# Loading and storing token tiles: one transfer over 128 partitions in place of four over 32

## The chip, the cores and the metric

The kernel runs on one core of a Trainium2 chip. The metric is the time of one execution on the device, in microseconds. The engines are named as in the profile: PE is TensorE (matmul), PEld its weight loads, DVE VectorE, ACT ScalarE, POOL GpSimd, SP the sync engine. In this kernel every transfer is issued by SP, and SP's own sequencer stands in the profile as SPq.

## What is computed

Two layers of a backbone over 1024 latent tokens and 256 context tokens of width 1024, in float32. Layer 0 is differential attention with rotary positions, layer 1 a bidirectional S5 state-space mixer with a GLU; each is followed by a squared-ReLU MLP of width 4096. Sublayers are wrapped in RMS norms and in shift, scale and gate from adaLN. Context reads only context; latent tokens read both. Cut to what matters here:

```python
for i in range(2):
    sh1, s1, g1, sh2, s2, g2 = split(silu(c) @ ada_w[i] + ada_b[i], 6)      # and the same from c_ctx for the context
    h = rmsnorm(x, norm_g[i, 0]) * (1 + s1) + sh1
    y = diff_attention(h, ...) if i == 0 else s5_mixer(h, ...)
    x = x + g1 * rmsnorm(y, norm_g[i, 1])
    h = rmsnorm(x, norm_g[i, 2]) * (1 + s2) + sh2
    x = x + g2 * rmsnorm(square(relu(h @ w1[i])) @ w2[i], norm_g[i, 3])
return x                                                                    # (1, 1024, 1024)
```

## The kernel before

The 1280 tokens stand in ten tiles of 128: tiles 0 to 7 are latent tokens, 8 and 9 context. A tile does not hold 128 neighbouring tokens. A token's number is written as c, sh (0 to 3) and sl (0 or 1), with token = 8 c + 2 sh + sl. Tiles 2p and 2p + 1 are a pair; the pair takes 32 values of c, and tile i takes sl = i mod 2. Partition 32 sh + j of a tile holds the j-th c of its pair with that sh. So the 32 rows for one sh are 8 tokens apart in DRAM, and the four blocks of 32 partitions start 2 tokens apart. A row of one token is 4 KB; in a pair both sl stand next to each other, so its rows are 8 KB.

Two helpers move such rows. `pair_dma` loads a pair, for `v_norm` at the start of the kernel. `tile_dma` loads or stores one tile of 128 rows. Each issues four transfers, one for each sh, of 32 partitions. All transfers of the kernel go through `self.dma` (L80), which issues them from SP in one queue.

The callers, in order of time:

- `v_norm` (called from `phase_v`): pairs 0 and 1 are loaded first, then 2 and 3, then the context pair 4. The rows are normalised (ACT L149, POOL L336), transposed on PE (`to_feature`, L314), scaled and shifted by the adaLN columns and split in a high and a low part; `mm3` (L132 to L134) multiplies them as three matmuls. The adaLN products (L249, L204) and the projection of V run at the same time.
- `phase_c`, after attention: the output projection. For each tile (in the order 8, 9, 0 to 7) `finish` loads the residual rows of x, adds them to the normalised projection (L1273), stores the sum to DRAM as `xa`, and normalises it once more for the MLP (L149, L1280). Three buffers `xs` hold the rows, in turn, so the load for a tile waits until the tile three places earlier is stored and read. Feature transposes of a group need all four of its tiles.
- `m0_tile`, at the end of the first MLP: `first` loads the rows of `xa`, `residual` (L1644) adds them and, for the latent tiles, stores the sum to `xb`; `second`, `root` and `modulate` (L1652) norm it for the next layer and write over the stored rows in place. Then `transposed` (L1619) lays the rows out for the S5 mixer, whose first product is at L1727; S5 also reads tables (`ptd`, `recd`) through the same queue. `glu_done` later loads `xb` by a transfer of its own, which the change does not touch.

A planner orders each engine's instructions ahead of time (`schedule_with_timeline_sim`), and an engine works them off in that order. Eight semaphores are used in turn for the transfers, so a transfer is issued only when the one eight places earlier has landed.

Of the kernel before, what the change touches and what calls it, by code (L numbers as in the profile page):

```python
# [70 lines left out]
class Prog:  # L71
# [206 lines left out]
    def tile_dma(self, dram, i, slot, store=False):  # L278

        d = dram[1] if i >= 8 else dram[0]  # L280
        src = d.rearrange("(c sh sl) d -> sl sh c d", sh=4, sl=2)[i % 2]
        if i < 8:
            src = src[:, 32 * (i // 2) : 32 * (i // 2) + 32]
        for sh in range(4):
            s = slot[32 * sh : 32 * sh + 32]
            if store:
                self.dma(src[sh], s)
            else:
                self.dma(s, src[sh])

    def pair_dma(self, dram, pair, slot):

        src = (dram[1] if pair == 4 else dram[0]).rearrange("(c sh sl) d -> sh c (sl d)", sh=4, sl=2)
        if pair < 4:
            src = src[:, 32 * pair : 32 * pair + 32]
        for sh in range(4):
            self.dma(slot[32 * sh : 32 * sh + 32].rearrange("p a b -> p (a b)"), src[sh])

    G_TOK = (512, 512, 256)
    G_TILES = ((0, 1, 2, 3), (4, 5, 6, 7), (8, 9))  # L300
# [1964 lines left out]
```

## Time and profile before

| | |
|---|---|
| median of 3 runs | 2943.51 us (2942.1 to 2946.0) |
| the profiled execution | 2951.44 us, span 2949.7 us |
| mean granted TensorE clock | 0.981 |
| PE, PEld, DVE, ACT, POOL busy | 95%, 78%, 64%, 44%, 34% of the span |
| transfers of SP's queue | 510.11 MB, 55.7% of 16 DMA engines' span |
| mean rate of all transfers | 174 GB/s |

How to read the lines that follow. A row of the stretches ("4.00:12.50 ...") gives the stretch in us from the span's start, its length, then busy us and (in brackets) instructions of PE, PEld, DVE, ACT and POOL, then the granted PE clock, the mean busy share of the 16 DMA engines and GB/s. A row of the timeline gives start, duration in us, engine, line, operation, out<-in, and in square brackets how long the engine had been idle and what released it. A row of one line's instructions gives count, then min/median/max in ns and the first and last start in us. A row of the waits gives who waited for whom, us in total, times and the longest. A row of the chain gives start, us, and the work that held the end.

### The profile page before, as it was taken

What the parts mean: (1) busy time and instruction counts of PE and PEld (TensorE: products, weight loads), DVE (VectorE), ACT (ScalarE), POOL (GpSimd) and SP (SyncE); (2) the same over time, 40 slices, a digit from 0 to 9 for tenths busy, and PEclk for the clock granted to TensorE, in tenths of its full rate; (3) what the DMA queues carried; (4) which work ended last, traced back from release to release, by engine and by line L of the source; (5) the groups of instructions that cost most, each with busy time, mean ns of one, the idle gap of its engine ahead of it and who ended that gap; (6) DMA issues with size and microseconds to landing.
All of it is one profiled execution on the core that took longest, in us unless ns stands there. A gap on an engine that the chain in (4) does not pass through costs nothing.

```text
span 2949.7 us, 44385 instructions
## 1 busy us (share of the span) xinstructions
PE 2795.1 (95%) x16040; PEld 2315.4 (78%) x16040; DVE 1877.9 (64%) x2777; ACT 1309.8 (44%) x2412; POOL 1016.2 (34%) x911
## 2 busy tenths in 40 slices
PE   6998999999899999999999999779899999999999
PEld 4687888888777887888777778678788778888887
DVE  5356788878763654444578764888633676658466
ACT  3424556555553743233422231357434655345443
POOL 2214676666653600000100001677301334326324
PEclk9999999999899999999999999989999999999999
DMA  9954455454625445322566674569934475467544
GB/s 269 300 193 141 129 156 154 153 156 146 217 86 177 138 152 185 125 97 86 194 173 186 183 238 119 150 184 278 287 121 154 151 234 189 151 205 263 161 137 140
DMA packets 422920, 512.95 MB, mean 174 GB/s; under 512 B 57142, under 2 KB 295980, under 8 KB 421548
## 3 DMA queue, kind: packets, MB, share of 16 engines
q1 hardware_dynamic: 422700, 510.11, 55.7%
q8 instruction: 126, 2.06, 0.3%
q14 instruction: 94, 0.77, 0.1%
HBM read 351.29 MB, written 154.50 MB: 171 GB/s over the span
## 4 chain that ended last, share of the span: by engine, by line
PE 55%; DVE 6%; DMA 5%; ACT 3%; issue 2%; SPq 2%; POOL 1%; DVEq 0%; POOLq 0%; ACTq 0%
PE PS L132 17%; PE PS L134 17%; PE PS L133 17%; SPq L80 2%; PE PS L1727 1%; DVE FD L1747 1%; DMA U<-in_ada_w 1%; DVE H L138 1%; DMA W<-in_mlp_w 1%; DMA H<-xb 1%; PE PS L204 1%; PE PS L1768 0%; ACT F L552 0%; DMA W<-recd 0%; DVE F L542 0%
## 5 line engine op out<-in xcount | busy, mean ns | idle before, releaser
L132 PE MATMUL PS<-H,R 128*128 128x512 f32 (+1 forms) x816 | 302.9, 374 | 8.3 <-DVE FC L468 5.8
L132 PE MATMUL PS<-H 128*128 128x512 f32 x768 | 300.3, 392 | 3.9 <-ACT H L137 3.9
L134 PE MATMUL PS<-H 128*128 128x512 f32 x768 | 299.4, 391 | 1.6 <-DVE H L138 1.6
L133 PE MATMUL PS<-H 128*128 128x512 f32 x768 | 300.8, 392 | 0.0
L133 PE MATMUL PS<-H,R 128*128 128x512 f32 (+1 forms) x816 | 293.9, 360 | 1.4 <-POOL H L138 1.4
L134 PE MATMUL PS<-H,R 128*128 128x512 f32 (+1 forms) x816 | 293.8, 361 | 0.0
L132 PE MATMUL PS<-R,H 128*128 128x512 f32 x540 | 217.5, 406 | 2.0 <-ACT R L137 1.4
L552 ACT ACTIVATE F<-F,stat 128x1280 f32<-128x1280 f32 x128 | 174.3, 1362 | 100.8 <-DVE F L542 100.6
L137 ACT ACTIVATE R<-W 128x512 fp32r<-128x512 f32 (+1 forms) x186 | 133.1, 721 | 193.2 <-PE PS L133 149.4
L134 PE MATMUL PS<-R,H 128*128 128x512 f32 x540 | 211.7, 396 | 1.8 <-DVE H L138 1.8
L133 PE MATMUL PS<-R,H 128*128 128x512 f32 x540 | 213.3, 396 | 0.0
L138 DVE TENSOR_TENSOR H<-W,H 128x512 fp32r<-128x512 f32 (+1 forms) x145 | 136.7, 951 | 109.6 <-ACT H L137 102.5
L542 DVE TENSOR_SCALAR_CACHE_REDUCE F<-PS 128x1280 f32<-128x1280 f32 x128 | 185.1, 1482 | 18.5 <-PE PS L517 18.5
L589 POOL TENSOR_SCALAR R<-F 128x256 fp32r<-128x256 f32 (+1 forms) x128 | 135.8, 1061 | 162.2 <-ACT F L588 144.6
L138 DVE TENSOR_TENSOR R<-W,R 128x512 fp32r<-128x512 f32 (+1 forms) x149 | 126.0, 851 | 102.9 <-ACT R L137 81.7
L137 ACT ACTIVATE H<-W 128x512 fp32r<-128x512 f32 (+2 forms) x166 | 107.1, 653 | 178.8 <-PE PS L133 117.9
L132 PEld LDWEIGHTS PS<-H,R 128*128 128x128 f32 x816 | 154.9, 190 | 37.2 <-DVE FC L468 7.4
L517 PE MATMUL PS<-R,R 64*128 64x256 f32 (+1 forms) x1380 | 160.4, 351 | 21.8 <-DVE F L542 7.5
L134 PEld LDWEIGHTS PS<-H,R 128*128 128x128 f32 x816 | 154.7, 190 | 26.4 <-POOL R L138 1.4
L133 PEld LDWEIGHTS PS<-H,R 128*128 128x128 f32 x816 | 155.5, 191 | 22.7 <-POOL H L138 1.7
L132 PEld LDWEIGHTS PS<-H 128*128 128x128 f32 x768 | 144.4, 188 | 36.5 <-ACT H L137 4.7
L134 PEld LDWEIGHTS PS<-H 128*128 128x128 f32 x768 | 144.5, 188 | 32.4 <-DVE H L138 2.1
(450 smaller groups left out, 7230.0 us busy)
## 6 DMA issues: line engine op xcount, KB each, us to landing
W<-in_mlp_w SPq DMA_DIRECT2D x192, 256.0 KB
Ad<-F SPq DMA_DIRECT2D x112, 256.0 KB
W<-Ad SPq DMA_DIRECT2D x112, 256.0 KB
W<-in_ada_w SPq DMA_DIRECT2D x32, 512.0 KB
W<-in_mlp_w SPq DMA_DIRECT2D x32, 512.0 KB
H<-hidd SPq DMA_DIRECT2D x64, 256.0 KB
U<-in_ada_w SPq DMA_DIRECT2D x32, 512.0 KB
W<-in_s_w_glu SPq DMA_DIRECT2D x64, 256.0 KB
```

Source lines behind the costliest of these rows:

```text
L80: return self.nc.sync.dma_start(out=out, in_=in_)
L132: mm(out, ah, bh, start=first, stop=False, **kw)
L133: mm(out, ah, bl, start=False, stop=False, **kw)
L134: mm(out, al, bh, start=False, stop=last, **kw)
L137: self.nc.scalar.activation(hi, src, AF.Copy)
L138: (lo_eng or self.nc.vector).tensor_tensor(lo, src, hi.bitcast(F32), ALU.subtract)
L204: self.nc.tensor.matmul(acc[32 * j : 32 * j + 32, 0:256], self.scT[:, 2 * k : 2 * k + 32], w[:, 256 * j : 256 * j + 256], start=k == 0, st ...
L517: mm(self.PS[:, o : o + k1 - k0], Q[rows, i, qs], K[j][rows, k0:k1], start=n == 0, stop=n == 2)
L542: ts(p[c], self.PS[:, 1280 * c : 1280 * c + 1280], 1.0, None, ALU.mult, ALU.min, accum_out=sm[:, c : c + 1])
L552: nc.scalar.activation(p[c], p[c], AF.Exp, bias=sm[:, c : c + 1], scale=-1.0, accum_out=sn[:, 0:1] if c else s0[:, u + 1 : u + 2])
L589: nc.gpsimd.tensor_scalar(hi, t, 1.0, 0.0, ALU.mult, ALU.add)
L1727: mm(b[:, o : o + 160], X[:, d, i, 64 * j : 64 * j + 128], U[:, 4 * n + i, cols], start=True, stop=True)
```

## The change

`tile_dma` and `pair_dma` issue one transfer for all 128 partitions. The DRAM side is a pattern of [4 values of sh][32 values of c][row], the SBUF side the whole buffer of 128 partitions. Buffers, callers and everything else stay as they are.

```diff
@@ tile_dma
         if i < 8:
             src = src[:, 32 * (i // 2) : 32 * (i // 2) + 32]
-        for sh in range(4):
-            s = slot[32 * sh : 32 * sh + 32]
-            if store:
-                self.dma(src[sh], s)
-            else:
-                self.dma(s, src[sh])
+        if store:
+            self.dma(src, slot)
+        else:
+            self.dma(slot, src)
@@ pair_dma
         if pair < 4:
             src = src[:, 32 * pair : 32 * pair + 32]
-        for sh in range(4):
-            self.dma(slot[32 * sh : 32 * sh + 32].rearrange("p a b -> p (a b)"), src[sh])
+        self.dma(slot.rearrange("p a b -> p (a b)"), src)
```

## The prediction

> **What bounds the kernel now.** I read the page first, then the list of transfers, then short windows of the DMA engines, then the waits and the chain in the three places where the changed helpers run.
>
> ```profile
> span 2949.7 us, 44385 instructions
> PE 2795.1 (95%) x16040; PEld 2315.4 (78%) x16040; DVE 1877.9 (64%) x2777; ACT 1309.8 (44%) x2412; POOL 1016.2 (34%) x911
> PE 55%; DVE 6%; DMA 5%; ACT 3%; issue 2%; SPq 2%; POOL 1%; DVEq 0%; POOLq 0%; ACTq 0%
> ```
>
> PE is busy for 95% of the span and holds 55% of the chain that ended last; transfers have 5% and the sequencer that issues them 2%. So a cheaper transfer can win little, and only where PE stands still; a slower one costs whatever PE's cover doesn't take. The changed transfers are these (engine, count, KB of each):
>
> ```profile
> F<-in_x SPq DMA_DIRECT2D x16, 256.0 KB
> FC<-in_ctx SPq DMA_DIRECT2D x4, 256.0 KB
> W<-in_x SPq DMA_DIRECT2D x20, 128.0 KB
> xa<-W SPq DMA_DIRECT2D x28, 128.0 KB
> xa<-F SPq DMA_DIRECT2D x12, 128.0 KB
> H<-xa SPq DMA_DIRECT2D x24, 128.0 KB
> RD<-xa SPq DMA_DIRECT2D x16, 128.0 KB
> xb<-FD SPq DMA_DIRECT2D x32, 128.0 KB
> recd<-ktd SPq DMA_DIRECT2D x128, 32.0 KB
> ```
>
> With 12 more F<-in_x and 8 W<-in_ctx of 128 KB they are 172 issues, which become 43: five pair loads of 1 MB, ten tile loads and ten tile stores (`x0`, `xa`) in `phase_c`, ten tile loads and eight tile stores (`xa`, `xb`) around the end of the first MLP, all of 512 KB. The last row is not changed; I need it below.
>
> **The one thing that decides: on how many DMA engines a new transfer runs.** A transfer of today has 32 rows on both sides. A new one has 128 partitions on the SBUF side, but on the DRAM side the pattern `sh c d` has a slowest dimension of 4: four blocks of 32 rows that can't be merged, since `sh` steps 2 rows and `c` steps 8. The program already holds transfers whose slowest dimension is 4: `recd<-ktd` (4 x 16 rows of 512 B). Windows of 0.1 us, with the DMA share of 16 engines and GB/s at the end of the row, set them beside a store of today:
>
> ```profile
> 1525.66 19.56 SPq L80 DMA_DIRECT2D recd<-ktd  x32
> 1531.10:1531.20 0.10, 0.10 (x2) 0.10 (x1) 0.10 (x1) 0.10 (x1) 0.00 (x0) 1.00 0.18 46
> 1531.20:1531.30 0.10, 0.10 (x2) 0.05 (x2) 0.10 (x2) 0.04 (x1) 0.00 (x0) 1.00 0.27 82
> 1530.00:1545.00 15.00, 15.00 (x83) 11.90 (x82) 6.32 (x7) 0.77 (x2) 0.00 (x0) 1.00 0.21 54
> 1864.80:1864.90 0.10, 0.10 (x2) 0.10 (x1) 0.10 (x1) 0.10 (x1) 0.00 (x0) 1.00 1.08 246
> 1865.20:1865.30 0.10, 0.10 (x2) 0.06 (x2) 0.10 (x2) 0.07 (x2) 0.00 (x0) 1.00 1.34 287
> ```
>
> The store of today bursts over all 16 engines (1.08 and 1.34; a packet reaches beyond so short a slice, so it can pass 1) and is done. The slowest-dimension-4 transfers drip at 0.18 to 0.27, and at 0.21 over 15 us: a quarter of the engines, 4 of 16. So I take four engines for the new transfers, and each must move 128 KB of a tile or 256 KB of a pair instead of 32 or 64 KB.
>
> The Trainium skill ("DMA: Bandwidth & Descriptors", section on why a DMA increments its semaphore by 16) states that a transfer uses the largest number of engines, at most 16, that divides the slowest dimension of both sides; for 4 and 128 it would give 4. The rows above agree for 4 against 4; no run here yet shows 4 against 128.
>
> **Price of a row.** The rate of one busy engine is GB/s divided by 16 x share:
>
> ```profile
> 4.00:12.50 8.50, 0.43 (x2) 0.18 (x1) 2.12 (x11) 2.33 (x6) 0.00 (x0) 1.00 0.92 204
> 16.00:28.00 12.00, 9.70 (x133) 5.88 (x135) 0.93 (x5) 2.30 (x4) 5.28 (x8) 1.00 1.06 374
> 1848.50:1851.50 3.00, 3.00 (x15) 2.49 (x14) 3.00 (x3) 1.84 (x4) 1.78 (x3) 1.00 0.61 178
> 1864.50:1867.50 3.00, 3.00 (x15) 2.48 (x14) 1.93 (x2) 1.87 (x4) 1.67 (x4) 1.00 0.69 175
> ```
>
> That is 22.1 GB/s for wide weight loads (16 to 28 us), 18.2 for a tile load of today, 15.9 for a tile store of today, 13.9 for the pair loads of today (4 to 12.5 us). On four engines a tile (131 KB an engine) then takes 5.9, 7.2 or 8.3 us, and a pair (262 KB) 11.9 to 18.9 us. I take 7.2 us for a tile, the load's own row, which lies between the other two, and the middle, 15.4 us, for a pair, since four engines meet each other less often than 16. Today a tile's 0.52 MB takes about 3 us (at 175 to 178 GB/s) and a pair's 1.05 MB 5.1 us (at 204 GB/s). All transfers stand in one SP queue, so I count what is issued later as waiting behind them on those four engines.
>
> **Start (pair loads).**
>
> ```profile
> PE PS L314 <- DMA F<-in_x: 10.7, 1, 10.7
> 32.22 2.01 PE L132 MATMUL PS<-R,H 128*128 128x512 f32 x4 [0.32 <-ACT H L137]
> 41.96 5.76 SPq L80 DMA_DIRECT2D F<-in_x  x8
> 56.47 1.06 ACT L149 ACTIVATE F<-F 128x1024 f32<-128x1024 f32 x1 [2.38 <-DMA F<-in_x]
> 64.00:76.00 12.00, 12.00 (x73) 9.00 (x76) 9.86 (x42) 2.25 (x4) 0.00 (x0) 0.97 0.86 207
> 65.62 1.73 SPq L80 DMA_DIRECT2D FC<-in_ctx  x4
> ```
>
> PE waits 10.7 us for the first rows of x and starts products at 32.22; the adaLN and V weights are queued behind x. Pairs 0 and 1: 2 x 15.4 = 30.8 us of queue for 10.3 today: +20.5 (+13.5 to +27.5). Pairs 2 and 3 are issued from 41.96 and awaited until 56.47, 14.5 us, and ACT already waits for them: 30.8 - 14.5 = +16.3 (+9.3 to +23.3). The context pair has full PE work ahead of it (12.00 of 12 us): 15.4 against 5 us, of which I count 4 (0 to 14). Sum +40.8 (+22.8 to +64.8).
>
> **phase_c.**
>
> ```profile
> 943.30 5.31 SPq L80 DMA_DIRECT2D xa<-W  x8
> 980.93 1.70 SPq L80 DMA_DIRECT2D W<-in_x  x4
> L1273 DVE SCALAR_TENSOR_TENSOR W<-F,stat,W x7: 1285/1285/2303, 942.0 to 997.9; 128x1024 f32<-128x1024 f32 x7
>   POOL stat L144: 16.6, 10
> ```
>
> All ten residual adds (L1273) wait for POOL today (10 times, 16.6 us), none for a transfer: loads are covered. The last add is at 997.9. With three x buffers the load of tile i can't start before the store of the tile three places earlier has landed. From the first store at 943.3, stores of 8, 9, 0 to 4 and loads of 1 to 7 must pass before tile 7 can be added: 14 transfers of 7.2 us, so 1044.1: +46 (5.9: +28; 8.3: +62). Late next are RMS, the transposes of tiles 4 to 7 and the products behind them in PE's fixed order; DVE's in-order adds hold up PSUM evacuation meanwhile. I count no cover, as PE had no idle time for transfers here to give back.
>
> **End of the first MLP.**
>
> ```profile
> FD<-ptd SPq DMA_DIRECT2D x1, 1664.0 KB
> 1835.30 1.71 SPq L80 DMA_DIRECT2D H<-xa  x4
> 1896.83 0.42 SPq L80
> 1897.75 2.96 DMA H<-xa
> 1906.70 2.30 SPq L80 DMA_DIRECT2D H<-recd  x4
> 1922.01 1.29 DVE L1652 SCALAR_TENSOR_TENSOR FD<-U,tl,W 128x1024 f32<-128x1024 f32 x1 [1.40 <-DMA xb<-FD]
> PE PS L1727 <- issue: 22.3, 1, 22.3
> ```
>
> Here the chain runs through loads and stores: `modulate` (L1652) overwrites the rows that the store of `xb` reads, so it waits for the store, and PE stands still 22.3 us until S5 can begin. From 1835.3, eight loads and eight stores, 16 x 7.2 = 115.2 us, and some 4.6 MB of wide tables (ptd, recd) at 16 x 22.1 GB/s, 13 us, pass the four engines: 1963.5 instead of 1922.0: +41 (5.9: +21; 8.3: +59). What is saved here: three issues of 0.42 us at two places of the chain, 2.5 us. The other 120-odd issues lie off the chain (SPq has 2%).
>
> **Sum.** 40.8 + 46 + 41 - 2.5 = +125 us; low ends 22.8 + 28 + 21 - 2.5 = +69, high ends 64.8 + 62 + 59 - 2.5 = +183. The profiled execution took 2951.4 us (span 2949.7), 0.3% above the median of 2943.5; I set the difference on the median: 3068.5 us, +4.2%.
>
> **Rivals.**
> *All 16 engines (ends faster).* If the hardware spread the 128 SBUF partitions over 16 engines, rows would go at 22.1 GB/s an engine. Pairs 0 and 1 then take 2.1 MB / 353 GB/s = 5.9 us for 10.3, -4.4; pairs 2 and 3 as much, of which half shows, -2.2; the end saves 2.5 us of issue and about 1 us of transfer; `phase_c` is covered today and gains nothing: -10 us, 2933. It decides only above 4 engines: at 8 the tile takes 3.6 us and loads stay covered, about no change. For it speaks that one side counts 128; against it the 0.21. The Trainium skill's "Rules for kernel authors" on the same page wants one 128-partition transfer in place of several over fewer partitions; by that advice alone this rival would be right. Chance 6%.
>
> *Four engines, mostly covered.* Only the start's first pairs (+15) and the last four tiles (4 loads and 4 stores behind the tables, some +20) show, while PE finds other work in `phase_c` and for pairs 2 and 3: +35, 2979. For it: PE was full there; against it: its order is fixed. Chance 14%, with +6 to +69 as its span.
>
> *More than the transfers themselves.* The waits of the SP queue show a transfer held 5.7 us for an earlier one to land:
>
> ```profile
> SPq L80 <- DMA FD<-ptd: 5.7, 1, 5.7
> ```
>
> If one new transfer in four (ten of 43) holds the queue in this way for one more tile time of 7.2 us, 72 us come on top: +197, 3140. Chance 7%.
>
> **How the numbers follow.** The forecast (+69 to +183) has 70%, no visible change (8 engines, or all covered) 3%, the rivals 6, 14 and 7%. Measurement tells 0.2%, 5.9 us, from no change. Slower: 70 + 14 + 7 = 91%; same 3%; faster 6%. The range takes the forecast's span and half of the covered case below and some of the held case above: 2985 to 3135; the forecast's own is 3012 to 3127.
>
> **What would show it.** Right: transfers of 512 KB at a DMA share near 0.25 through 4 to 30 us and 943 to 1040 us; residual adds (L1273, L1644) released by W<-in_x or H<-xa in place of POOL; L1652 waiting for xb<-FD for tens of us; PE idle before the first product, near 1000 us, and before S5; the MLP and attention stretches between them unchanged. Wrong: bursts of share 1 for the new transfers, or PE's stops in these places no longer than before.

## The result and the profile after

The changed kernel takes 3084.58 us (median of 4 runs, 3071.17 to 3088.48) against 2944.76 us for the kernel before: a ratio of 1.0455, 95% interval 1.0439 to 1.0471, or +139.8 us. It is slower. The profiled execution is the fastest of the four, 3071.17 us, with a span of 3069.4 us, 119.7 us longer than the span of before; stage sums below are from it and so come out below the median's difference.

The page of the changed kernel: span, busy time, the chain by engine.

```profile
span 3069.4 us, 44166 instructions
PE 2812.0 (92%) x16040; PEld 2328.2 (76%) x16040; DVE 1877.6 (61%) x2777; ACT 1310.8 (43%) x2412; POOL 1009.5 (33%) x911
PE 48%; DMA 10%; DVE 6%; issue 3%; ACT 2%; SPq 2%; POOL 1%; DVEq 0%; POOLq 0%; ACTq 0%
```

PE's busy time grew by 16.9 us (2795.1 before), and the span by 119.7: most of what is lost is time in which PE stands still, and its share of the span fell from 95% to 92%. The 16.9 us go with a lower granted clock in the places where PE is stopped (0.82 in the window below, 1.00 before). On the chain, transfers rose from 5% to 10%.

Windows in the stage of the first residual adds, two of the changed kernel and then the whole stage before; then the residual add's own row (line numbers are 3 lower here: L1270 is L1273 of before) and its last two executions; then the waits that grew (who waited for whom, us, times, longest).

```profile
1002.00:1080.00 78.00, 55.11 (x245) 44.96 (x244) 20.45 (x23) 36.97 (x78) 37.73 (x54) 0.82 0.25 101
1012.00:1022.00 10.00, 5.53 (x26) 4.26 (x24) 0.69 (x1) 3.69 (x9) 5.67 (x9) 0.89 0.25 101
```

```profile
941.00:998.00 57.00, 52.84 (x276) 43.89 (x274) 23.04 (x26) 38.55 (x80) 44.93 (x59) 1.00 0.59 160
```

```profile
L1270 DVE SCALAR_TENSOR_TENSOR W<-F,stat,W x7: 1284/1285/2304, 1000.1 to 1080.8; 128x1024 f32<-128x1024 f32 x7
1071.85 1.28 DVE L1270 SCALAR_TENSOR_TENSOR F<-F,stat 128x1024 f32<-128x1024 f32 x1 [9.75 <-DMA F<-in_x]
1080.82 2.30 DVE L1270 SCALAR_TENSOR_TENSOR W<-F,stat,W 128x1024 f32<-128x1024 f32 x1 [1.49 <-POOL stat L144]
```

```profile
DVE FD L1649 <- DMA xb<-FD: 52.4, 7, 10.0
ACT F L149 <- DMA F<-in_x: 48.6, 3, 20.9
DVE W L1270 <- DMA W<-in_x: 26.0, 3, 9.6
```

The DMA share stands at 0.25 for 78 us on end, and at 0.25 in the ten of them taken alone, where the whole stage before had 0.59. The share is a mean over 16 engines; the packets in the trace show what is behind it: four of them run at once for 86% of the 78 us, and three or five for nearly all the rest. So one quarter of the engines works without a pause and three quarters do nothing. 101 GB/s over a quarter of 16 engines is 25.3 GB/s an engine. The last residual add moved from 997.9 to 1080.8 us. Four of the ten adds wait now for a load of x, 35.7 us in all, where before all waited for POOL alone; the last of the four is the add of tile 6 at 1071.85, and that of tile 7 follows it by 9.0 us, as it did before. Modulate (L1649, L1652 of before) waits 52.4 us for stores of xb; before, its row in the waits was

```profile
DVE FD L1652 <- DMA xb<-FD: 4.3, 3, 1.5
```

The start, from the timeline of the changed kernel: SP's issues, then ScalarE's squares (the first tile of pairs 0, 1 and 2 and of the context pair).

```profile
3.49 0.63 SPq L80 DMA_DIRECT2D F<-in_x  x1
4.70 0.56 SPq L80 DMA_DIRECT2D F<-in_x  x1
5.29 15.22 SPq L80 DMA_DIRECT2D W<-in_ada_w  x4
105.00 0.58 SPq L80 DMA_DIRECT2D FC<-in_ctx  x1
...
26.62 1.06 ACT L149 ACTIVATE F<-F 128x1024 f32<-128x1024 f32 x1 [20.89 <-DMA F<-in_x]
40.98 1.06 ACT L149 ACTIVATE F<-F 128x1024 f32<-128x1024 f32 x1 [11.93 <-DMA F<-in_x]
85.81 1.06 ACT L149 ACTIVATE F<-F 128x1024 f32<-128x1024 f32 x1 [15.78 <-DMA F<-in_x]
149.00 1.06 ACT L149 ACTIVATE F<-FC 128x1024 f32<-128x1024 f32 x1 [6.88 <-DMA phd<-F]
```

The same of before, as far as the prediction has not shown it:

```profile
7.82 4.71 SPq L80 DMA_DIRECT2D W<-in_ada_w  x4
...
12.30 1.06 ACT L149 ACTIVATE F<-F 128x1024 f32<-128x1024 f32 x1 [3.41 <-DMA F<-in_x]
16.92 1.06 ACT L149 ACTIVATE F<-F 128x1024 f32<-128x1024 f32 x1 [2.29 <-DMA F<-in_x]
97.02 1.06 ACT L149 ACTIVATE F<-FC 128x1024 f32<-128x1024 f32 x1 [7.60 <-DMA phd<-F]
```

Pairs 0 and 1 are there at 26.62 and 40.98 us in place of 12.30 and 16.92. Two things are to be seen beside that: four weight loads that took SP 4.71 us to issue take 15.22 us, and the context pair is issued at 105.00 us in place of 65.62.

How far each kernel's trace is behind that of before, in us, at four places: the first scores product (228.4 before), the last residual add of the first stage (997.9), the first S5 product (1924.3) and the end of the span (2949.7). The last column is the median against the runs of before on the same chip.

| kernel | first scores | last residual add | first S5 product | span | median |
|---|---|---|---|---|---|
| the change | +54.5 | +82.9 | +124.1 | +119.7 | +139.8 |
| pairs only | +56.3 | +58.2 | +57.3 | +54.4 | +59.3 |
| tiles only | +0.7 | +33.7 | +86.5 | +85.1 | +81.6 |
| quarters of the columns | +36.1 | +68.8 | +98.0 | +95.4 | +98.6 |
| halves | +94.7 | +198.4 | +337.5 | +332.6 | +339.0 |
| xa in tile order | +1.2 | +4.5 | +2.4 | +1.6 | +0.7 |
| xa and xb in tile order | +0.1 | -0.3 | -0.5 | -5.3 | +1.6 |
| the change, xb stored by four | +55.8 | +86.1 | +96.8 | +92.0 | +101.0 |
| context pair only | +13.0 | +10.1 | +8.8 | +8.7 | +13.5 |
| eighths | +9.1 | +28.3 | +24.3 | +22.6 | +22.6 |
| tiles only, xa in tile order | +1.1 | +8.8 | +43.4 | +40.3 | +46.4 |
| context pair only, from ScalarE's queue | +14.2 | +11.7 | +14.7 | +11.4 | +15.3 |

For the change: start +54.5, first residual stage +28.4, end of the MLP +41.2, and some 4 us given back in the S5 stretch. The attention stretch between (last scores product +51.5) and the MLP stretch (first residual add at its end +83.9) keep what they were given, within 4 us. With the tiles alone the MLP stretch does not: the first residual add at its end is at +45.7, 12.0 us more than the last add of the first stage. Why is open; the stages themselves are best compared from their own first add on, as is done below.

### The profile page after: what moved, and what is told of

The parts are those of the page before. It is cut to its first block, busy times and chain, and to the rows that moved or that the text cites. A ratio compares the mean times of both kernels' runs of the same rounds, so it can differ in the third digit from the quotient of the medians.

```text
span 3069.4 us, 44166 instructions
## 1 busy us (share of the span) xinstructions
PE 2812.0 (92%) x16040; PEld 2328.2 (76%) x16040; DVE 1877.6 (61%) x2777; ACT 1310.8 (43%) x2412; POOL 1009.5 (33%) x911
## 4 chain that ended last, share of the span: by engine, by line
PE 48%; DMA 10%; DVE 6%; issue 3%; ACT 2%; SPq 2%; POOL 1%; DVEq 0%; POOLq 0%; ACTq 0%
PE PS L132 15%; PE PS L133 14%; PE PS L134 14%; DMA xb<-FD 2%; SPq L80 2%; PE PS L1724 1%; DMA H<-hidd 1%; DMA xa<-W 1%; DMA U<-in_ada_w 1%; DVE FD L1744 1%; PE PS L1765 1%; DMA W<-in_mlp_w 1%; DVE H L138 1%; DMA RD<-xa 1%; PE PS L204 1%
## 5 line engine op out<-in xcount | busy, mean ns | idle before, releaser
L132 PE MATMUL PS<-R,H 128*128 128x512 f32 x540 | 216.2, 402 | 13.3 <-ACT H L137 11.7
L138 DVE TENSOR_TENSOR R<-W,R 128x512 fp32r<-128x512 f32 (+1 forms) x149 | 126.5, 854 | 98.6 <-ACT R L137 73.7
L132 PEld LDWEIGHTS PS<-H 128*128 128x128 f32 x768 | 145.4, 189 | 45.7 <-DVE FD L1463 5.0
```

The lines of the kernel that those rows point to most:

```text
L132: mm(out, ah, bh, start=first, stop=False, **kw)
L138: (lo_eng or self.nc.vector).tensor_tensor(lo, src, hi.bitcast(F32), ALU.subtract)
```

## The experiments

**Which half costs what.** The two helpers were changed one at a time.

```diff
 # pairs only: pair_dma
-        for sh in range(4):
-            self.dma(slot[32 * sh : 32 * sh + 32].rearrange("p a b -> p (a b)"), src[sh])
+        self.dma(slot.rearrange("p a b -> p (a b)"), src)
 # tiles only: tile_dma
-        for sh in range(4):
-            ...
+        if store:
+            self.dma(src, slot)
+        else:
+            self.dma(slot, src)
```

> Only the five pair loads of the start are one transfer each; tiles stay at four transfers of 32 partitions. Theory A (a transfer whose DRAM side has 4 as its slowest dimension runs on 4 DMA engines, each stage pays for itself): the start is late by what the trace of after shows at the first scores, about 51 us, the two later stages pay nothing: +45 to +55 us, 2989 to 3000 us. Rival B (the tile transfers later on cost through the queue that the late start shifts, so that the pairs alone cost little): under +25 us.

Measured 3007.24 us, ratio 1.0189 (1.0165 to 1.0213), +59.3 us; all of it is there at the first scores.

> Only the tile loads and stores (two residual stages) are one transfer each; the pairs stay at four. Theory A: the start is as before, the stage of the first residual adds pays about 31 us and the end of the MLP about 41 us: +65 to +75 us, 3009 to 3020 us, and with the pairs-only kernel the two add up to the whole change within 8 us. Rival B (stages interact: the late start widens the later ones): the two sum to less than 120 us of the 141.

Measured 3029.49 us, ratio 1.0260 (1.0234 to 1.0285), +81.6 us. The medians are above both expectations, which were read from the profiled execution of the change, the fastest of its four. Their sum is 140.9 us, against 139.8 for the whole change: by the medians each stage pays for itself, and the stages don't interact. (The profiled executions add up to 139.5 against 119.7; that of the tiles is the slowest of its four.) The tiles' cost stands where it stood in the change. From the first add of the first residual stage to its last 80.6 us pass (80.7 in the change, 55.9 before). From the first add at the end of the MLP to the first S5 product the kernel is 40.8 us slower than before (40.2 in the change); the rest of the 52.8 us between the two columns of the table are the 12.0 us of the MLP stretch.

**Engines, or the size of a transfer?** Two kernels keep more than one transfer but change the slowest dimension of the DRAM side.

```diff
 # quarters: tile_dma; pair_dma likewise with 512 columns
-        for sh in range(4):
-            s = slot[32 * sh : 32 * sh + 32]
+        for q in range(4):
+            s, x = slot[:, 256 * q : 256 * q + 256], src[:, :, 256 * q : 256 * q + 256]
 ...
 # halves
+        for h in range(2):
+            s, x = slot[64 * h : 64 * h + 64], src[2 * h : 2 * h + 2]
```

> Again four transfers for a tile or pair, each of all 128 partitions and a quarter of the columns: as many transfers of as many bytes as before, but the DRAM side is 4 x 32 x 256 elements (4 x 32 x 512 for a pair), 4 slowest. Theory A (4 engines): as slow as after or slower, since each packet is 1 KB (2 KB) and costs more for a byte: +130 to +230 us, 3075 to 3175 us, DMA share near 0.25 in the residual stages. Rival C (what costs is one large transfer in place of four: nothing of a tile is there before its last row, and one issue holds the queue): like before, within 15 us, 2930 to 2960 us.

Measured 3046.50 us, ratio 1.0322 (1.0303 to 1.0341), +98.6 us.

> Two transfers of 64 partitions for a tile or pair: the DRAM side is 2 x 32 x 1024 (2 x 32 x 2048), 2 slowest. Theory A (2 engines): a tile takes about twice the 5.15 us of after, 10.3 us, a pair 20 to 30; the residual stage +31 + 14 x 5.15 = about +100, the end of the MLP +41 + 12 to 16 x 5.15 = +100 to +125, the start +100 to +150: +300 to +375 us, 3245 to 3320 us, DMA share near 0.125 in the residual stages. Rival C (size of a transfer): between before and after, +30 to +100 us, 2975 to 3045 us.

Measured 3286.94 us, ratio 1.1143 (1.1116 to 1.1170), +339.0 us. The windows of the residual stage, first of the quarters, then of the halves:

```profile
985.00:1062.00 77.00, 51.30 (x223) 42.13 (x222) 18.32 (x22) 35.96 (x75) 32.65 (x51) 0.84 0.27 95
```

```profile
1055.00:1190.00 135.00, 49.80 (x210) 40.16 (x209) 17.28 (x20) 31.38 (x66) 32.34 (x48) 0.67 0.13 52
```

Quarters, with as many transfers as before and up to four of a tile queued at once, stand at 0.27, four engines; halves stand at 0.13, two. The rate of a busy engine is 25.0 GB/s with halves (52 over 16 x 0.13) against 25.3 in the change: the engines work as fast, there are only fewer. With quarters it is 22.0 (95 over 16 x 0.27), with rows of 1 KB in place of 4 KB. That several such transfers together don't rise above a quarter says that they share the same four engines. The Trainium skill ("DMA: Bandwidth & Descriptors", section on why a DMA increments its semaphore by 16) states the largest divisor up to 16 of both slowest dimensions, and the lowest-numbered engines where there are fewer than 16; for a slowest dimension of 4 or 2 against 128, 64 it gives 4 and 2, and these rows agree in the number; which four engines they are, the rows don't show.

The quarters missed their expectation on the low side: +98.6, where at least +130 was expected. The engines are as few, so the 41 us below the change are what one large transfer costs more than four small ones on the same four engines. The traces show 30 us of it, at the start (+36.1 for +54.5) and at the end of the MLP (+29.2 for +41.2); the first residual stage gains nothing (+32.7 for +28.4). The timeline of the quarters, SP and the squares of pair 0, shows how:

```profile
4.68 12.27 SPq L80 DMA_DIRECT2D F<-in_x  x7
...
12.33 1.06 ACT L149 ACTIVATE F<-F 128x1024 f32<-128x1024 f32 x1 [2.16 <-DMA F<-in_x]
17.81 1.06 ACT L149 ACTIVATE F<-F 128x1024 f32<-128x1024 f32 x1 [4.24 <-DMA F<-in_x]
```

The first tile of pair 0 is complete after two of its four transfers, at 12.33 us (26.62 in the change), and the weight loads, issued behind seven more transfers that took SP 12.27 us, come too late to share the four engines with it. Which of the two weighs more was not separated.

**One large transfer on 16 engines.** The scratch tensors can be kept in the order of the tiles; then a tile is 128 rows in a line.

```diff
-                self.tile_dma(self.xa, i, x, store=True)
+                self.dma(self.xa[i], x)
-            self.tile_dma(self.xa, i, x)
+            self.dma(x, self.xa[i])
-            self.xa = dt("xa0", 1024, 1024), dt("xa1", 256, 1024)
+            self.xa = dt("xa0", 10, 128, 1024)
 # second kernel also: xb0 as 8 x 128 x 1024, stored by one transfer, and in glu_done
-            self.dma(x, self.xb[0].rearrange("(c t) d -> t c d", t=8)[t])
+            sh, sl = t // 2, t % 2
+            for p in range(4):
+                self.dma(x[32 * p : 32 * p + 32], self.xb[2 * p + sl][32 * sh : 32 * sh + 32])
```

> The kernel before, with the scratch xa kept in the order of the tiles (10 x 128 x 1024), so that each of its loads and stores is one transfer over 128 partitions whose DRAM side is 128 rows in a line; pairs, x tiles and xb as before. Theory A (the slowest dimension of the DRAM side sets the engines): 16 engines, so no loss and a few issues less: -4 to +2 us, 2942 to 2949 us, DMA share not held at 0.25. Rival C (one large transfer costs in itself, with its end landing late): half of the tile transfers are such, so about half of the tiles-only kernel's 82 us, +25 to +45 us.

Measured 2948.49 against 2947.75 us, ratio 1.0005 (0.9996 to 1.0014).

> As the one before, and xb in tile order too, stored by one transfer; its later reader, the GLU's load, then needs four transfers of 32 partitions (24 issues more near 2200 us, 24 stores' issues less near 1900 us). Theory A: 16 engines everywhere: -8 to +2 us, 2938 to 2949 us; a stage near 2200 us that has no gap to fill hides the extra issues. Rival C: about all of the tile stages' 82 us less the ten x loads, +45 to +65 us.

Measured 2949.33 us, ratio 1.0005 (0.9995 to 1.0015). No difference that can be measured, in either direction: a 512 KB transfer over 128 partitions costs nothing by itself here when it has the engines, so in these stages the size counts only together with the four engines. Nor is there a gain: the first of the two issues 60 transfers fewer, and no time comes back. Neither beats the kernel before.

**Inside the end of the MLP.** The forecast priced this stage as a queue of 16 transfers; the trace showed modulate waiting for the store of the rows that it overwrites. One kernel takes the stores out of the four engines, the other the loads of xa.

```diff
 # the change, xb stored by four transfers
-                self.tile_dma(self.xb, i, y, store=True)
+                dst = self.xb[0].rearrange("(c sh sl) d -> sl sh c d", sh=4, sl=2)[i % 2]
+                for sh in range(4):
+                    self.dma(dst[sh, 32 * (i // 2) : 32 * (i // 2) + 32], y[32 * sh : 32 * sh + 32])
 # tiles only, with the xa lines of the diff above
```

> The changed kernel, with the xb stores alone put back to four transfers of 32 partitions. Theory A1 (of the 41 us that the end of the MLP pays, most is modulate waiting for the xb store of its own tile, as the 52.4 us over 7 waits say): the stage pays 5 to 15 us, the whole is 3050 to 3062 us. Rival A2 (as the forecast had it: the queue of 16 transfers in a row sets the end, so that with half of them gone 8 x 5.15 = 41 us of loads lie beside the work): the stage pays about nothing to 5 us, 3043 to 3050 us. Rival A3 (the xa loads on four engines are what sets the end): within 8 us of after, 3076 to 3092 us.

Measured 3048.70 us, ratio 1.0345 (1.0329 to 1.0360). The stage pays 10.7 us at the first S5 product and 5.9 at the end of the span, as theory A1 has it, but the whole time falls 1.3 us outside its range, into A2's: this kernel does not decide between the two. A3 is out.

> The tiles-only kernel with xa in tile order, so that only the x loads (10 tiles, the seven later ones in the residual stage) and the xb stores (8 tiles) still run on 4 engines. Theory A1 (the end of the MLP pays because modulate overwrites the tile that its xb store still reads, and waits 10 us for it): that wait stays, somewhat shorter without xa loads ahead in the queue: the end pays 20 to 35 us; the first residual stage, with 7 x 5.15 = 36 us of transfers in its 57 us, pays 0 to 10 us: +20 to +45 us, 2968 to 2993 us. Rival A2 (the row of 16 or 14 transfers on four engines sets each stage's end, as forecast): with half of them gone both stages fit, 0 to +10 us, 2948 to 2958 us.

Measured 2994.51 us, ratio 1.0163 (1.0146 to 1.0181), +46.4 us. The waits of modulate, with the loads of xa on four engines and the stores on 16, then with the stores on four and the loads on 16, and three of its rows in the second one's timeline:

```profile
DVE FD L1651 <- DMA xb<-FD: 12.4, 6, 5.0
```

```profile
DVE FD L1650 <- DMA xb<-FD: 47.4, 8, 9.0
```

```profile
1875.40 1.28 DVE L1650 SCALAR_TENSOR_TENSOR FD<-FD,tl,W 128x1024 f32<-128x1024 f32 x1 [9.00 <-DMA xb<-FD]
1888.06 1.28 DVE L1650 SCALAR_TENSOR_TENSOR FD<-FD,tl,W 128x1024 f32<-128x1024 f32 x1 [7.78 <-DMA xb<-FD]
1900.69 1.28 DVE L1650 SCALAR_TENSOR_TENSOR FD<-FD,tl,W 128x1024 f32<-128x1024 f32 x1 [9.02 <-DMA xb<-FD]
```

With half of the transfers off the four engines, the wait keeps 47.4 us and the stage still pays 34.6 us (43.4 - 8.8). A full queue does not explain that; eight stores that DVE waits out one by one do. The change itself says the same, in a window of this stage:

```profile
1950.00:1980.00 30.00, 18.57 (x65) 14.14 (x65) 13.08 (x11) 5.75 (x10) 8.74 (x12) 0.87 0.14 39
```

At 0.14 the four engines stand still for nearly half of the time, and PE works for 18.57 of 30 us. In the kernel with the loads on 16 engines the tiles come 12.6 us apart (1875.40, 1888.06, 1900.69), 8 to 9 of which are the wait. The first residual stage, with only the x loads on four engines, pays 7.7 of 33 us. The total is 1.4 us above A1's upper end, and far from A2's.

**The context pair alone.** Forecast at 4 us; the trace of the change showed 13 to 14 us between the first adaLN product and the first scores.

```diff
 # pair_dma
+        if pair == 4:
+            self.dma(slot.rearrange("p a b -> p (a b)"), src)
+            return
 # second kernel: self.nc.scalar.dma_start(out=..., in_=src) there
```

> The kernel before, with only the context pair loaded by one transfer. Theory S1 (in the trace of after ctx is late because its issue is late, 105.0 us against 65.6 us, held behind the earlier loads on SP's queue; its own four engines are covered): within 5 us of before, and its first squares near 97 to 100 us. Rival S2 (its own four engines are what makes the 14 us between the first ada product and the first scores): +8 to +16 us, squares after 105 us.

Measured 2961.23 us, ratio 1.0051 (1.0034 to 1.0067), +13.5 us. S1 falls: issued at 65.26 us, as early as before, the pair still costs 13. S2's size is right, but what is waited for is not the pair's own rows. The timeline of the kernel with the context pair alone, SP, then the end of PE's longest stop there and the squares, and a window of it:

```profile
65.26 0.63 SPq L80 DMA_DIRECT2D FC<-in_ctx  x1
71.12 11.43 SPq L80 DMA_DIRECT2D Vd<-R  x4
102.30 0.35 SPq L80 DMA_DIRECT2D phd<-F  x1
...
85.56 1.08 PE L204 MATMUL PS<-W,scT 128*32 128x256 f32 x8 [11.40 <-DMA W<-in_ada_w]
109.53 1.06 ACT L149 ACTIVATE F<-FC 128x1024 f32<-128x1024 f32 x1 [8.17 <-DMA phd<-F]
```

```profile
71.00:83.00 12.00, 3.16 (x29) 2.05 (x27) 3.12 (x10) 2.62 (x5) 2.48 (x2) 0.78 0.42 116
```

and the same place in the kernel before:

```profile
73.25 2.32 SPq L80 DMA_DIRECT2D Vd<-R  x4
90.34 0.41 SPq L80 DMA_DIRECT2D phd<-F  x1
```

```profile
71.00:83.00 12.00, 12.00 (x80) 9.25 (x79) 6.33 (x14) 6.05 (x10) 5.13 (x4) 1.00 0.86 256
```

Four stores of V that come behind the context pair took SP 11.43 us to issue in place of 2.32. Those stores hold the buffers that ScalarE and DVE write V's rows to:

```profile
DVE R L379 <- DMA Vd<-R: 17.7, 2, 13.5
ACT R L378 <- DMA Vd<-R: 12.4, 2, 11.2
```

Before, the same two waits were 4.4 and 1.5 us. And the store of phd, on which the squares wait, is issued 12.0 us later. PE falls from 12.00 to 3.16 us of work in these 12 us, and what it waits for, 11.40 us, is an adaLN weight load. The packets show why: of the 128 rows of the load issued at 66.00 us, right behind the pair, 96 run before 70 us and 32, a quarter, from 82 to 85 us, when the pair's rows are through. A quarter of 16 engines is four, as many as the pair holds.

> The ctx-only kernel, with that one load issued from ScalarE's queue in place of SP's. Theory S3 (the 13 us came through SP's queue: with the ctx load outstanding four issues of Vd stores took 11.43 us in place of 2.32, and the store of phd, on which the squares wait, was issued at 102.30 in place of 90.34 us): SP's issues are as before, 0 to +4 us, 2948 to 2952 us. Rival S4 (the four engines themselves are held by ctx rows, and every transfer that has rows on them lands late whoever issues ctx): +8 to +14 us, 2956 to 2962 us.

Measured 2963.39 us, ratio 1.0054 (1.0039 to 1.0069), +15.3 us: S3 falls, and S4's size holds with 1.3 us over its range. In this kernel the context pair is not in SP's queue at all; its timeline with the end of PE's longest stop, and then the row of the V stores' issues from 60 to 104 us (min/median/max in ns):

```profile
64.37 1.17 ACTq L297 DMA_DIRECT2D FC<-in_ctx  x1
70.26 10.59 SPq L80 DMA_DIRECT2D Vd<-R  x4
88.91 0.80 PE L132 MATMUL PS<-R,H 128*128 128x512 f32 x1 [11.71 <-DVE R L379]
```

```profile
L80 SPq DMA_DIRECT2D Vd<-R x8: 359/414/8635, 70.3 to 89.7; - x8
```

SP is held just as long, 8.635 us in one single issue. The same row with the pair in SP's queue, and before:

```profile
L80 SPq DMA_DIRECT2D Vd<-R x8: 371/534/8740, 71.1 to 89.2; - x8
```

```profile
L80 SPq DMA_DIRECT2D Vd<-R x13: 365/506/2085, 73.3 to 103.1; - x13
```

So the hold of SP is not the order of one queue; it goes with the engines that the large transfer fills. Nor does the turn of the eight semaphores show in it: SP's only wait for the context pair itself is 2.4 us in this kernel, ahead of a later weight load. S4's "every transfer that has rows on them lands late" is not what happened, though. From another queue the pair lets the adaLN weights through (PE waits 1.30 us for them in place of 11.40), and PE stands still 11.71 us all the same, now for VectorE, which waits up to 14.8 us for a V store. There are two ways from the pair to PE, each of nearly the same length, and taking one of them away wins nothing. The Trainium skill ("DMA: Bandwidth & Descriptors", section "Rules for kernel authors") says that spreading transfers over issuing engines gives no bandwidth and only saves time of the sequencer; here the first part agrees (+15.3 us against +13.5), and the second did not come (four issues take 10.59 us against 11.43).

**The other direction.**

```diff
+        for q in range(8):
+            s, x = slot[16 * q : 16 * q + 16], src[q // 2, 16 * (q % 2) : 16 * (q % 2) + 16]
```

> The other direction: eight transfers of 16 partitions for a tile or pair, DRAM side 16 x 1024 (16 x 2048), 16 slowest, as before on 16 engines, one row for each; some 170 issues more, at 0.42 us each 71 us more of SP's queue. Theory I (SP's issues lie beside other work, so their number, up or down, moves little; what moved the time was the engines alone): within 10 us of before, 2938 to 2958 us. Rival J (issues are on the path at the start and in the residual stages, so that saving them was a real gain that the four engines ate): +15 to +40 us, 2963 to 2988 us.

Measured 2970.74 us, ratio 1.0076 (1.0060 to 1.0093), +22.6 us: J's size, and not I's. 9.1 us of it are there at the first scores; 16 issues of pairs 2 and 3 hold SP for 13.74 us there, where eight held it 5.76:

```profile
45.85 13.74 SPq L80 DMA_DIRECT2D F<-in_x  x16
```

The rest lies in the first residual stage, whose adds wait 13.0 us for loads of x, and at the end of the MLP: the last add of the first stage is at +28.3, the MLP stretch gives 9.8 us of that back (first add at its end +18.5), and the end of the MLP pays 5.8. Whether the number of issues or the sixteen-row transfers themselves cause that part stays open. The kernels in tile order saved issues of xa and xb and gained nothing; that added issues cost shows here at the start alone.

## Why the prediction was right

**Four engines.** Right, and the step on which all else rests: 0.25 in the change, 0.27 with quarters, 0.13 with halves, and no cost with 128 rows in a line. The rival of 16 engines is out.

**The price of a tile.** Too high. The forecast took 7.2 us with 5.9 as the low end, from rows in which 16 engines were busy together; four alone ran at 25.3 GB/s, which is 131 KB / 25.3 = 5.2 us. The price of a pair was right: the context pair alone moved 67 GB/s on four engines (last section), 15.6 us for 1.05 MB, where 15.4 was taken as the middle between two rows.

**phase_c.** Forecast +46 (28 to 62), measured +28.4 in the change and +33 with the tiles alone. The queue was as full as the forecast had it (0.25 for 78 us), and the term of the sum that was mis-sized is the 7.2 us: 14 x 5.2 us from 943.3 would have ended at 1016.1, only 18 us late. From first add to last the stage took 24.8 us longer than before (80.7 for 55.9). Of the 6.6 us more, 3.8 stand at the end: the last add does not follow the fourteenth transfer, as the forecast had it, but tile 6's add, by 9.0 us in place of one transfer's 5.2. The others were not separated. The rest of the 28.4 (3.6 us, and 8.3 of the 33 with the tiles alone) is there before the stage's first add; its cause is open.

**Start.** Forecast +40.8, measured +54.5. Pairs 0 to 3 were well priced: the first product of V moved by 23.5 us (32.2 to 55.7) for 20.5 forecast, the first adaLN product of L204 by 40.9 (57.4 to 98.3) for 36.8. The step that failed is the context pair, "of which I count 4 (0 to 14)": it looked at who waits for the context rows and found them covered, and not at who waits for the stores issued after them. It measured 13 to 15 us alone, by the stores and by the adaLN weights issued right behind it.

**End of the MLP.** Forecast +41 (21 to 59), measured +41.2, in the right place and with the wait of L1652 that it named. But the working was a full queue from 1835.3 on, with 13 us of tables in it, and that is not what happened: the share is 0.14 where the queue should have been full, eight stores alone cost 34.6 us and the loads alone 6 to 11. That the size agreed is luck. The saved 2.5 us of issue were not to be seen.

**Sum.** +125 forecast, +119.7 in the profiled execution and +139.8 in the medians: a price too high in one stage and a cover that did not hold in another nearly cancel, which is luck; the four engines and the three places are not. *Mostly covered* is out: PE had no work to put into phase_c, where it fills 55.11 of 78 us (52.84 of 57 before). Of *more than the transfers themselves* a part came true: SP held for 15.22 us over four weight loads is a cost of this kind. In phase_c issues are held too (two of xa take 6.30 us), but the four engines work there without a pause, so that a held issue adds nothing; no run shows it as 72 us on top, on one transfer in four.

## What to carry to other kernels

Before several transfers are made one, look at the slowest dimension of both sides: a pattern of few blocks on the DRAM side turns 128 partitions into as few engines as there are blocks (4 and 2 here), and the DMA share in a window of the trace (0.25 here) says so at once. If one transfer is wanted, lay the DRAM tensor out so that the 128 rows are its slowest dimension; and expect nothing from fewer issues unless a view shows SP's issue on the path. Price a slow transfer by what is issued behind it and by who overwrites what it reads, and not only by who reads what it brings.

## What the runs showed of the hardware that was not expected

A large transfer on four engines holds the issue of later transfers, also from another queue: one store of V took 8.74 us to issue behind the context pair in SP's queue and 8.635 us with that pair in ScalarE's, while the longest such issue before was 2.085 us in the same stretch. And the four engines are not equally fast everywhere: pairs 0 and 1, issued at 3.49 us with weight loads behind them, were complete at 40.98 us, 37 us for 2.1 MB or 56 GB/s, where the tiles of the residual stage moved 101 GB/s on as many engines. The weight loads are at most a part of that. In the kernel with the context pair alone, its packets are the only ones from 75 to 81 us:

```profile
75.00:81.00 6.00, 0.00 (x0) 0.00 (x0) 0.00 (x0) 0.05 (x1) 2.09 (x2) 0.72 0.25 67
```

At the same share of 0.25 they move 67 GB/s, 16.8 an engine against 25.3 for the tiles. A pair's rows are 8 KB and a tile's 4 KB; whether that is the reason was not measured.
